# Hybrid encoder block, fp32 by split matmuls: w_o's Strassen groups end with P3, P4 in place of P4, P3, and three smaller moves of work on DVE and ACT

## The chip, the cores and the metric

The kernel runs on one core of a Trainium2 chip. The metric is the device time of one execution in microseconds. Before the change three runs took 2060.41, 2061.68 and 2065.68 us; the median is 2061.68. The engines are called as the profile calls them: PE is TensorE, DVE is VectorE, ACT is ScalarE, POOL is GpSimd, SP is SyncE, which issues most transfers.

## The reference

One layer of a streaming encoder on 1024 tokens of width 1024, all in fp32:

```python
def reference(x, ...):
    for l in range(DEPTH):
        h = h + FFN_RES_WEIGHT * swiglu_ffn(rmsnorm(h, norm_ffn1[l]), ffn1_w_in[l], ffn1_w_out[l])
        u = rmsnorm(h, norm_mix[l])
        ...
        h = h + W_o(sum_b sigmoid(gate_b) * branch_b)
        h = h + 0.5 * SwiGLU_2(RMSNorm(h))
    Final RMSNorm
```

(The last three lines stand in the reference's own words.) The mixing takes q, k, v, two gates and a pooling input from one projection of u; one branch is retention with rotary q and k and decay by head, the other a multi-scale trailing mean. `W_o` is a product of 1024 x 1024 with the merged branches. SwiGLU has an inner width of 2816.

## The kernel before

**Products.** Every fp32 operand is kept as a hi and a lo part (`split`, and `split_scaled` where a gain is folded in; lines 164 to 169), and one product is three matmuls, hi by hi (L184), hi by lo (L185) and lo by hi (L186). Tiles are 128 partitions by 512 tokens.

**Strassen groups.** The large products are made in 2 x 2 blocks of weights and operands by seven products in place of eight (`strassen`, from L470). Each of the seven is 4 blocks of k, so 12 matmuls. Their names here: P1 = L11 R11 and P2 = L12 R21 go into bank `a`; P6 = S2 T2, P5 = S1 T1 and P3 = S4 R22 go into bank `b`, which ACT starts with a copy of P1 (L529); P7 = S3 T3 and P4 = L22 T4 go into bank `e`. L and S are blocks of the weights or sums of them, R and T the same of the operand. Results leave the banks as follows: ACT copies `b` after P6 (the `v` of L534) and `e` after P7 (the `p7` of L551); output block (0,0) is `a` after P2, (1,1) is `b` after P5 plus p7, (0,1) is `b` after P3, and (1,0) is `e` after P4 plus v. There are two banks for `b` and six others.

**Order.** `two_by_two` runs two groups side by side, product by product. The order of the seven is a tuple of indices:

```python
BY_OPERAND = (0, 4, 1, 3, 2, 6, 5)
```

which reads P1, P2, P6, P7, P5, P4, P3. Weight preparation runs up to four steps ahead (`LOOK`). The other work (squares, operand sums T1 to T4, splits of operands, sums of norms) is put into a queue (`Flow`), of which two items are taken at each step. A scheduler then fixes the order in which each engine's instructions stand. DVE and ACT take them strictly as they stand there.

**w_o.** The stage has two pairs of groups, wo0 with wo1 and wo2 with wo3. The operand of the first is `mg`, the merged branches; it is made while the pair ru2, ru3 of the mixing's up-projections ends. `handed` decides which operand blocks are prepared after which product. `evac` takes the banks into `wo` tiles; for some blocks POOL adds h by a transfer (`onto`, L143), and the block's square for the norm of SwiGLU2 (named n3) is queued afterwards (`quarter`, then ACT's square, L291, and DVE's add into `n3ssq`, L303). After w_o, `stats` makes the norm's sums: PE adds over the partitions (`n3sum`), `inverse_root` takes the root (ACT, L241) and refines it on DVE, and `spread` makes rows of it. The result is the operand of SwiGLU2's first product, whose weight tiles are called c.

**Buffers.** Raw weight tiles (`ra`, `rb`, each 1024 wide and 0.5 MB) have four buffers; a new load goes out when the oldest one's last reader has finished. Split weights have five.

**Other places of the change.** `values` makes the product with w_v; in its loop over k, DVE makes sums of weights (L1332 to L1334) and their splits `vS1w` and `vS2w`. `rotary_tables` loads the cos and sin tables. ACT's functions lie in tables that are loaded when another is needed; there are ten loads in the program, among them L216 and L1190 at its start, L241 at each norm's root, L796 at the first SiLU and L1261 at the first sigmoid of the gates, which lies in the stretch of the tiles p1 and t1.

Of the kernel before, what the change touches and what calls it, by code (L numbers as in the profile page):

```python
# [10 lines left out]
F32 = mybir.dt.float32  # L11
F32R = mybir.dt.float32r  # L12
BF16 = mybir.dt.bfloat16
AF = mybir.ActivationFunctionType
# [3 lines left out]
P = 128  # L18
# [32 lines left out]
N_MV, N_T4, N_RAW, N_WT, N_TL, N_C2 = 28, 9, 4, 5, 4, 8  # L51
LOOK = 4

BY_OPERAND = (0, 4, 1, 3, 2, 6, 5)


class Flow:
# [28 lines left out]
    def add(self, *work):  # L86
        self.back.extend(work)
# [3 lines left out]
def block_kernel(ctx: ExitStack, tc, x, x_tok, x_two, vecs, f1_in, f1_out, w_in, w_v, pool_w, w_ret, w_pool, w_o,  # L91
# [8 lines left out]
    flow = Flow()  # L100
# [22 lines left out]
    def tl(name):  # L123
        return sb.tile([P, S], F32, tag="tl", bufs=N_TL, name=name)
# [24 lines left out]
    def spill(name, n, width=S):  # L149
        return [dr.tile([P, width], F32, tag=f"{name}{i}", name=f"{name}{i}") for i in range(n)]  # L150

    def half(t, j):
        return t[:, j * H : (j + 1) * H]
# [126 lines left out]
    class Norm:  # L280


        turns = False

        def __init__(self, name):
            self.name, self.ssq, self.seen = name, None, set()
# [6 lines left out]
        def square(self, mt, tokens, src):  # L293
            if self.ssq is None:
                self.ssq = t4(f"{self.name}ssq")
            dst = self.ssq[:, tokens]
            if tokens.start not in self.seen:
                self.squared(dst, src)
                self.seen.update(range(tokens.start, tokens.stop, HD))
            else:  # L300
                q = c2(f"{self.name}q{mt}_{tokens.start}")[:, : tokens.stop - tokens.start]
                self.squared(q, src)
                tt(dst, dst, q, ADD)  # L303

    class Next(Norm):
# [139 lines left out]
                for i in range(4):  # L445
                    flow.add(lambda f=f, i=i: f(i))

        def stats(self, sums=None, between=(), diagonals=None):
            def roots():
                t = sums if sums is not None else token_sums(self.ssq, range(8), self.name)  # L450
                self.r_tok = inverse_root(t, D, self.name)

            def row(q):
                if not q:
                    self.row = t4(f"{self.name}rb")
                to, b = half(self.row, q), spread(self.r_tok[:, 4 * q : 4 * q + 4], f"{self.name}{q}", diagonals)
                if sums is not None:
                    to, b = in_row(to), in_turns(b)
                copy(to, b)
                if q:  # L460
                    self.rb = self.row

            n = max(0, len(between) - 3)
            flow.add(roots, *between[:n], lambda: row(0), *between[n:], lambda: row(1))
# [722 lines left out]
        flow.until(lambda: stored.issuperset(names))  # L1187

    def rotary_tables():
        act(warm, warm, AF.Sigmoid)  # L1190
        for n, z in (("cos", 0), ("sin", 1)):
            tab[n] = t4(n)
            load(tab[n], rope[z])
            tt(tab[n], tab[n], mix.rms(), MUL)
# [108 lines left out]
    def values():  # L1303

        nx, kept, two, p1s = mix, {}, {}, {}

        def fetch(r, *rows):

            for z, (k, o) in enumerate(rows):
                load(half(r, z), w_v[k, :, o * H : (o + 1) * H])  # L1310
            return half(r, 0), half(r, 1)

        def rows(n, k):

            if (n, k // 2) not in two:
                at, o = k // 2 * 2 + (4 if n[2] == "2" else 0), (1 if n[1] == "2" else 0)
                two[n, k // 2] = fetch(raw(f"v{n}{k}"), (at, o), (at + 1, o))
            return two[n, k // 2][k % 2]

        def block(n, k):  # L1320

            if n[0] == "L":
                return rows(n, k)
            if n in ("S1", "S3"):
                return two.pop((n, k))

            L11 = rows("L11", k)
            if n == "S4":
                tt(L11, rows("L12", k), L11, SUB)
                return L11  # L1330
            L21, L22 = fetch(tl(f"v{n}{k}"), (k, 1), (k + 4, 1))
            tt(L22, L21, L22, ADD)  # L1332
            tt(L21, L11, L21, SUB)
            tt(L11, L22, L11, SUB)  # L1334
            two["S1", k], two["S3", k] = L22, L21
            return L11

        bk = {}

        def step(L, R, k, where, start, after):  # L1340
            w = []

            def prep():
                t = weights(block(L, k), f"v{L}w{k}")
                w.extend(in_turns(flat(t, z)) for z in range(2))

            def body():
                if start and k == 0:
                    for i in range(4):
                        bk[where, i] = (sum_bank if where == "b" and i < N_SUM else bank)(f"v{L}{i}")  # L1350
                m = nx.operand(R, k)
                for i in range(4):
                    mm3(bk[where, i], parts(m, slice(i * P, (i + 1) * P)), w, start and k == 0, k == 3)
                    if k == 3:
                        with soon():
                            after(i, bk[where, i])

            return prep, body

        def store(o, j, i, src):  # L1360
            to = vs[2 * o + j].rearrange("p (h t c) -> p h t c", h=2, t=4)
            load(to[:, :, i], src.rearrange("p (h c) -> p h c", h=2))
            if i == 3:
                stored.update(f"v{h}{j}" for h in (2 * o, 2 * o + 1))

        def keep(n, i):
            if i % 2 == 0:
                kept[n, i // 2] = t4(f"v{n}{i}")
            return half(kept[n, i // 2], i % 2)

        def old(n, i):
            return half(kept[n, i // 2], i % 2)

        def result(o, j, other=None):
            def after(i, b):
                c = c2(f"vc{o}{j}{i}")
                if other is None:
                    copy(c, b)
                else:
                    tt(c, b, other(i), ADD)  # L1380
                flow.add(lambda: store(o, j, i, c))
                if (o, j, i) == (0, 0, 3):
                    nx.stats(between=nx.blocks("R22", [("tl", N_TL)] * 3, True))

            return after

        def after1(i, b):
            p1s[i] = c2(f"vp1{i}")
            copy(p1s[i], b)

        def after6(i, b):
            copy(keep("h", i), b)

        def after5(i, b):
            copy(keep("f", i), b)

        def product(L, R, where, start, f):
            return [step(L, R, k, where, start, f) for k in range(4)]

        yield from product("L11", "R11", "a", True, after1)  # L1400
        s2, s1 = product("S2", "T2", "a", False, after6), product("S1", "T1", "b", True, after5)
        nx.work(nx.t3)
        for k in range(4):
            if k == 2:
                nx.work(nx.r21, nx.t4_)
            yield (lambda a=s2[k], b=s1[k]: (a[0](), b[0]())), s1[k][1]
            yield (lambda: None), s2[k][1]
        for p in zip(product("S4", "R22", "b", False, result(0, 1, lambda i: old("h", i))),
                     product("S3", "T3", "a", False, result(1, 1, lambda i: old("f", i)))):
            yield from p  # L1410
        yield from product("L12", "R21", "b", True, result(0, 0, lambda i: p1s.pop(i)))
        yield from product("L22", "T4", "a", False, result(1, 0))
# [438 lines left out]

        return [group(n, i) for n, i in enumerate(at)]

    waiting = []

    def out_group(i):
        pair = [None, None]
# [26 lines left out]

        return lambda: strassen(mg, w_o[i], w_o[i + 4], name, evac, none, begin)

    def handed(nx, last):

        f = after(nx)

        def between(pair, n):
            if n in (3, 5):
                flow.add(*waiting)
                waiting.clear()
            if pair == 0:
                if n == BY_OPERAND[-1]:
                    flow.add(*(lambda m=m, i=i: m(i) for i in range(2) for m in (nx.r22, nx.sum1, nx.sum3)))
                return
            flow.add(*(lambda i=i: f[n](i) for i in range(2)))

            for m in {3: (0,), 6: (4,)}.get(n, ()):
                flow.add(*(lambda i=i: f[m](i) for i in range(2, 4)))
            if n == BY_OPERAND[-1]:
                rest = [lambda m=m, i=i: f[m](i) for m in (1, 3, 2, 6, 5) for i in range(2, 4)]
                last(rest)

        return between

    def merge():
        yield from two_by_two(two_groups(0) + two_groups(1), BY_OPERAND, handed(mg, lambda rest: flow.add(*rest)))  # L1910
        yield from two_by_two((out_group(i) for i in range(4)), BY_OPERAND,
                              handed(ffn2, lambda rest: (flow.add(*rest[:4]), ffn2.stats(between=rest[4:]))))

    ffn2 = Next("n3", V_FFN2, h2)
    ops2 = spill("r2", FH), spill("t2", FH), spill("b2", FH), spill("m2", FH, H)

    class Last(Norm):
# [193 lines left out]
```

## Time and profile before

| what | value |
|---|---|
| median of 3 runs | 2061.68 us |
| the profiled execution | 2062.72 us |
| its span | 2060.9 us |
| granted clock of PE | 0.999 |
| w_o, 1375 to 1450 us: PE, DVE, ACT busy | 73.47, 71.60, 48.29 of 75.00 us |
| the rest up to 1375: PE busy | 472.19 of 475.00, then 894.99 of 900.00 |
| from 1450 on: PE, DVE busy | 599.90, 548.67 of 611.00 us |

The profile is one execution. Busy time is what an engine worked; matmuls overlap, so a busy PE need not be at its peak, and a matmul's listed duration (0.38 us) is longer than the step from one to the next. In the timeline a row has the start, the duration, engine, line, operation, `out<-in`, shapes, and in brackets the time that the engine idled before it with what released it. Buffer numbers are left out of names there.

### The profile page before, as it was taken

To read this page: it belongs to the slowest core of one execution; us is meant where nothing else is said; L and a number is where in the kernel's file an instruction comes from. 1 tells how busy PE (TensorE), PEld (TensorE's weight loads), DVE (VectorE), ACT (ScalarE), POOL (GpSimd) and SP (SyncE) were. 2 spreads that over 40 slices of the span, in tenths; PEclk is the share of its full clock that TensorE was granted. 3 is DMA by queue.
4 is the path that set the end of the run, shared out by engine and by line. 5 is a ranking of instruction groups with operands and counts; after the bars stand their busy time and mean duration, and the time that the engine had idled before them with its cause. 6 is when DMAs were issued, how large, how long until landed. Compare 5 with 4: busy or idle time off the path is not lost.

```text
span 2060.9 us, 29728 instructions
## 1 busy us (share of the span) xinstructions
PE 2040.5 (99%) x10672; PEld 1810.4 (88%) x10672; DVE 1831.2 (89%) x3253; ACT 1092.5 (53%) x2066; POOL 9.1 (0%) x14
## 2 busy tenths in 40 slices
PE   9999999999999999999999999999999999999998
PEld 7888999988888888888888999888889989998887
DVE  8889998998996798989789987899989989899896
ACT  8545454554754554454447753456645545455454
POOL 0000000000000000000000000010000000000000
PEclk9999999999999999999999999999999999999999
DMA  6332424585543333243337667545223232368642
GB/s 245 137 103 77 143 88 143 199 274 196 187 146 109 107 136 110 85 151 119 117 125 229 203 227 278 185 109 163 82 98 133 88 133 88 135 208 274 211 148 97
DMA packets 120260, 313.57 MB, mean 152 GB/s; under 512 B 13361, under 2 KB 17585, under 8 KB 120113
## 3 DMA queue, kind: packets, MB, share of 16 engines
q1 hardware_dynamic: 118096, 308.01, 43.9%
q0 software_dynamic: 1440, 2.62, 0.8%
q8 instruction: 83, 1.36, 0.3%
q10 hardware_dynamic: 576, 1.05, 0.1%
q14 instruction: 65, 0.52, 0.1%
HBM read 220.93 MB, written 90.70 MB: 151 GB/s over the span
## 4 chain that ended last, share of the span: by engine, by line
PE 81%; DVE 12%; DMA 2%; ACT 2%; issue 2%; SPq 0%; ACTq 0%; DVEq 0%
PE c_b L185 2%; PE c_b L184 2%; PE c_b L186 2%; PE a_b L184 2%; PE a_b L186 2%; PE a_b L185 2%; PE c_e L186 2%; PE c_e L184 2%; PE c_e L185 2%; PE a_e L186 1%; PE a_e L184 1%; PE a_e L185 1%; PE a_a L186 1%; PE a_a L185 1%; PE a_a L184 1%
## 5 line engine op out<-in xcount | busy, mean ns | idle before, releaser
L184 PE MATMUL c_b<-n3T,c_wS 128*128 128x512 f32 x176 | 66.8, 380 | 1.7 <-ACT n3T L164 1.7
L185 PE MATMUL c_b<-n3T,c_wS 128*128 128x512 f32 x176 | 66.8, 380 | 0.0
L186 PE MATMUL c_b<-n3T,c_wS 128*128 128x512 f32 x176 | 66.7, 379 | 0.0
L184 PE MATMUL a_b<-n1T,a_wS 128*128 128x512 f32 x168 | 63.7, 379 | 0.0
L185 PE MATMUL a_b<-n1T,a_wS 128*128 128x512 f32 x168 | 63.7, 379 | 0.0
L186 PE MATMUL a_b<-n1T,a_wS 128*128 128x512 f32 x168 | 63.7, 379 | 0.0
L184 PE MATMUL a_a<-n1R,a_wL 128*128 128x512 f32 x120 | 45.5, 379 | 0.0
L186 PE MATMUL a_a<-n1R,a_wL 128*128 128x512 f32 x120 | 45.5, 379 | 0.0
L185 PE MATMUL a_a<-n1R,a_wL 128*128 128x512 f32 x120 | 45.5, 379 | 0.0
L184 PE MATMUL c_a<-n3R,c_wL 128*128 128x512 f32 x112 | 42.7, 381 | 0.7 <-ACT c_b L529 0.5
L185 PE MATMUL c_a<-n3R,c_wL 128*128 128x512 f32 x112 | 42.4, 379 | 0.0
L186 PE MATMUL c_a<-n3R,c_wL 128*128 128x512 f32 x112 | 42.4, 379 | 0.0
L184 PEld LDWEIGHTS c_b<-n3T,c_wS 128*128 128x128 f32 x176 | 33.3, 189 | 6.6 <-ACT n3T L164 2.1
L185 PEld LDWEIGHTS c_b<-n3T,c_wS 128*128 128x128 f32 x176 | 33.3, 189 | 4.8 <-DVE n3T L165 0.3
L186 PEld LDWEIGHTS c_b<-n3T,c_wS 128*128 128x128 f32 x176 | 33.3, 189 | 4.7
L186 PEld LDWEIGHTS a_b<-n1T,a_wS 128*128 128x128 f32 x168 | 31.8, 189 | 4.5
L185 PEld LDWEIGHTS a_b<-n1T,a_wS 128*128 128x128 f32 x168 | 31.8, 189 | 4.4
L184 PEld LDWEIGHTS a_b<-n1T,a_wS 128*128 128x128 f32 x168 | 31.8, 189 | 4.4
L165 DVE TENSOR_TENSOR a_wS<-a_S,a_wS 128x512 fp32r<-128x512 f32 x45 | 30.7, 684 | 3.8 <-ACT a_wS L164 3.8
L165 DVE TENSOR_TENSOR c_wS<-c_S,c_wS 128x512 fp32r<-128x512 f32 x46 | 31.2, 681 | 2.6 <-ACT c_wS L164 2.6
L164 ACT CAST a_wS<-a_S 128x512 fp32r<-128x512 f32 x45 | 27.3, 621 | 11.7 <-PE a_a L186 6.1
L184 PE MATMUL c_e<-n3T,c_wS 128*128 128x512 f32 x88 | 33.5, 380 | 0.0
(3167 smaller groups left out, 8012.2 us busy)
## 6 DMA issues: line engine op xcount, KB each, us to landing
c_ra<-in_f_in SPq DMA_DIRECT2D x22, 512.0 KB, 3.6
c_rb<-in_f_in SPq DMA_DIRECT2D x22, 512.0 KB, 3.5
a_ra<-in_f_in SPq DMA_DIRECT2D x21, 512.0 KB, 3.7
a_rb<-in_f_in SPq DMA_DIRECT2D x21, 512.0 KB, 3.7
t<-au SPq DMA_DIRECT2D x11, 512.0 KB, 3.5
b<-ag SPq DMA_DIRECT2D x11, 512.0 KB, 4.1
r<-au SPq DMA_DIRECT2D x11, 512.0 KB, 3.7
bra<-in_f_out SPq DMA_DIRECT2D x11, 512.0 KB, 5.5
```

Of the source, the lines that this page charges most:

```text
L164: copy(hi, src)
L165: tt(lo, src, hi.bitcast(F32), SUB)
L184: mm(dst, w[0], m[0], start=start, stop=False, skip_group_check=True)
L185: mm(dst, w[0], m[1], start=False, stop=False, skip_group_check=True)
L186: mm(dst, w[1], m[0], start=False, stop=stop, skip_group_check=True)
```

## The change

Four things are changed.

1. w_o's groups run P1, P2, P6, P7, P5, P3, P4 (`BY_TURN`). `handed` and the new `settled` order the operand work by that: after P3 of the last pair T2 and T3 of the operand's blocks 2 and 3 are queued, and after P4 R21, R22, T1 and T4. For the hand-over from the mixing to w_o, whose groups still end with P4, P3, the splits of R22 of blocks 0 and 1 are queued after T2 and T3 rather than ahead of them.
2. Squares of w_o's blocks for n3 go into spare halves of other tiles (`aside`); DVE's adds of them are kept back in a list, of which two are queued after P1, P2, P6 and P5 of the second pair and the others at the end, one at a time, ahead of the norm's sums.
3. In `values` the R21 and T4 work of the next operand is queued after the loop over k and not in its third turn.
4. `stats` lets ACT evaluate one column of the norm's inverse with the function that is needed next (`then`: SiLU, for the mixing's norm the sigmoid). The sigmoid of a dummy tile in `rotary_tables` goes. ACT's program has nine table loads in place of ten.

The diff's core:

```diff
-BY_OPERAND = (0, 4, 1, 3, 2, 6, 5)
+BY_OPERAND, BY_TURN = (0, 4, 1, 3, 2, 6, 5), (0, 4, 1, 3, 2, 5, 6)
...
+            elif self.aside:
+                self.aside(mt, tokens, dst, src)
...
                 self.r_tok = inverse_root(t, D, self.name)
+                act(sb.tile([P, 8], F32, tag="st", bufs=10, name=f"{self.name}f")[:, :1], self.r_tok[:, :1], then)
...
     def rotary_tables():
-        act(warm, warm, AF.Sigmoid)
...
         for k in range(4):
-            if k == 2:
-                nx.work(nx.r21, nx.t4_)
             yield (lambda a=s2[k], b=s1[k]: (a[0](), b[0]())), s1[k][1]
             yield (lambda: None), s2[k][1]
+        nx.work(nx.r21, nx.t4_)
...
+    def aside(mt, tokens, dst, src):
+
+        if not spare:
+            q = tl(f"n3q{mt}_{tokens.start}")
+            spare.extend((half(q, 1), half(q, 0)))
+        q = spare.pop()
+        ffn2.squared(q, src)
+        apart.append(lambda: tt(dst, dst, q, ADD))
+
+    def add(n):
+        for _ in range(min(n, len(apart))):
+            apart.popleft()()
...
-            flow.add(*(lambda i=i: f[n](i) for i in range(2)))
-
-            for m in {3: (0,), 6: (4,)}.get(n, ()):
-                flow.add(*(lambda i=i: f[m](i) for i in range(2, 4)))
-            if n == BY_OPERAND[-1]:
-                rest = [lambda m=m, i=i: f[m](i) for m in (1, 3, 2, 6, 5) for i in range(2, 4)]
-                last(rest)
+            if nx is ffn2 and n in (0, 4, 1, 2):
+                flow.add(lambda: add(2))
+            if n != 5:
+                flow.add(*(lambda i=i: f[n](i) for i in range(2)))
+
+            for m in {3: (0,), 6: (4,), 5: (1, 3) if order[-1] != 5 else ()}.get(n, ()):
+                flow.add(*(lambda i=i, m=m: f[m](i) for i in range(2, 4)))
+            if n == order[-1]:
+                rest = [lambda m=m, i=i: f[m](i) for m, at in ((1, 2), (3, 2), (5, 0), (2, 2), (6, 2), (5, 2))
+                        for i in (at, at + 1)]
+                last(rest if n == 5 else rest[4:])
...
+        flow.add(more, *rest[:2])
+        ffn2.stats(between=rest[2:])
...
-        yield from two_by_two((out_group(i) for i in range(4)), BY_OPERAND,
-                              handed(ffn2, lambda rest: (flow.add(*rest[:4]), ffn2.stats(between=rest[4:]))))
+        yield from two_by_two((out_group(i) for i in range(4)), BY_TURN, handed(ffn2, settled, BY_TURN))
```

Three places show how instructions move. First DVE at the hand-over to w_o, before; `wo0wS2` and `wo1wS2` are the lo halves of the S2 weights that P6 of wo0 and wo1 read, `mgT2*` and `mgT3*` are splits of T2 and T3, `mgR22*` of R22, and the `ru` rows make the T sums:

```order
L165 TENSOR_TENSOR wo0wS2_13645<-wo0S2_13643,wo0wS2_13645 128x512
L351 TENSOR_TENSOR ru20_13292<-ru21_13294,mgt12_13667 128x512
L351 TENSOR_TENSOR ru30_13328<-ru31_13330,mgt13_13673 128x512
L492 TENSOR_TENSOR wo1S1_13679<-wo1rb_13563 128x512
L165 TENSOR_TENSOR mgT22_13670<-ru20_13292,mgT22_13670 128x512
L165 TENSOR_TENSOR mgT23_13676<-ru30_13328,mgT23_13676 128x512
L492 TENSOR_TENSOR wo1S2_13681<-wo1S1_13679,wo1ra_13562 128x512
L351 TENSOR_TENSOR ru20_13292<-ru21_13294,ru20_13292 128x512
L351 TENSOR_TENSOR ru30_13328<-ru31_13330,ru30_13328 128x512
L165 TENSOR_TENSOR wo1wS2_13683<-wo1S2_13681,wo1wS2_13683 128x512
```

The same stretch of DVE now:

```order
L165 TENSOR_TENSOR wo0wS2_13654<-wo0S2_13652,wo0wS2_13654 128x512
L165 TENSOR_TENSOR mgT32_13677<-ru20_13295,mgT32_13677 128x512
L353 TENSOR_TENSOR ru30_13331<-ru31_13333,ru30_13331 128x512
L495 TENSOR_TENSOR wo1S1_13684<-wo1rb_13566 128x512
L508 TENSOR_TENSOR wo0rb_13543<-wo0ra_13542,wo0rb_13543 128x512
L165 TENSOR_TENSOR mgT33_13681<-ru30_13331,mgT33_13681 128x512
L495 TENSOR_TENSOR wo1S2_13686<-wo1S1_13684,wo1ra_13565 128x512
L165 TENSOR_TENSOR mgR220_13710<-ru01_12945,mgR220_13710 128x512
L165 TENSOR_TENSOR mgR221_13713<-ru11_12988,mgR221_13713 128x512
L165 TENSOR_TENSOR mgT12_13734<-mgt12_13638,mgT12_13734 128x512
L165 TENSOR_TENSOR wo1wS2_13688<-wo1S2_13686,wo1wS2_13688 128x512
```

Before the row of `wo1wS2` stand now T3's splits, wo0's S3 (`wo0rb`), R22 and one split of T1; counted from the row that takes (0,1) of ru3 (`ru3h01<-ru3b`), it has moved from the 17th to the 21st place.

Second, PE where P5 of wo1 ends, before:

```order
L186 MATMUL wo1b<-mgT_13731,wo1wS_13786 128x512
L184 MATMUL wo1b<-mgT_13734,wo1wS_13786 128x512
L185 MATMUL wo1b<-mgT_13734,wo1wS_13786 128x512
L186 MATMUL wo1b<-mgT_13734,wo1wS_13786 128x512
L184 MATMUL wo0e<-mgT_13586,wo0wL_13803 128x512 [waits Activation_49]
L185 MATMUL wo0e<-mgT_13586,wo0wL_13803 128x512
```

and now:

```order
L186 MATMUL wo1b<-mgT_13734,wo1wS_13789 128x512
L184 MATMUL wo1b<-mgT_13737,wo1wS_13789 128x512
L185 MATMUL wo1b<-mgT_13737,wo1wS_13789 128x512
L186 MATMUL wo1b<-mgT_13737,wo1wS_13789 128x512
L184 MATMUL wo0b<-mgR_13710,wo0wS_13807 128x512 [waits DVE_49,Activation_49]
L185 MATMUL wo0b<-mgR_13710,wo0wS_13807 128x512
```

P3 of wo0 (`wo0b<-mgR`, R22) has come to the place of P4 (`wo0e`, L22). It writes the bank that P5 of wo0 wrote just ahead of these rows, and its first matmul waits for DVE.

Third, DVE from the evacuation of (1,1) of the last pair on, now (`c0` and `c11` are the first weights of SwiGLU2):

```order
L1888 TENSOR_TENSOR wo21_13982<-wo2b_13997,wo2p7_14137 128x512
L165 TENSOR_TENSOR wo3wL22_14194<-wo3rb_13912,wo3wL22_14194 128x512
L1888 TENSOR_TENSOR wo31_14011<-wo3b_14026,wo3p7_14164 128x512
L165 TENSOR_TENSOR c0_wL11_14221<-c0_ra_14217,c0_wL11_14221 128x512
L495 TENSOR_TENSOR c11_S1_14326<-c11_rb_14240 128x512
L1894 TENSOR_TENSOR wo20_13980<-wo2b_13997,wo20_13980 128x512
L165 TENSOR_TENSOR c11_wL11_14243<-c11_ra_14239,c11_wL11_14243 128x512
```

The last reader of wo3's rb, whose buffer c11's rb takes, is the second row, and the reader of c11's rb the fifth. Before the change the reader stood 18 rows behind the evacuation of wo3, and that buffer was freed well ahead of it. The splits of T2's block 2 (`n3T22`) stood 37 rows behind that evacuation and stand now 15 behind it.

More of the change, by code (lines that the diff above doesn't have):

```diff
@@ L280, in block_kernel @@
     class Norm:
-        turns = False
+        turns, aside = False, None
         def __init__(self, name):
@@ L446, in work, with stats @@
                     flow.add(lambda f=f, i=i: f(i))
-        def stats(self, sums=None, between=(), diagonals=None):
+        def stats(self, sums=None, between=(), diagonals=None, then=AF.Silu):
             def roots():
@@ L1382, in after @@
                 if (o, j, i) == (0, 0, 3):
-                    nx.stats(between=nx.blocks("R22", [("tl", N_TL)] * 3, True))
+                    nx.stats(between=nx.blocks("R22", [("tl", N_TL)] * 3, True), then=AF.Sigmoid)
             return after
@@ L1852, in two_groups @@
         return [group(n, i) for n, i in enumerate(at)]
-    waiting = []
+    waiting, spare, apart = [], [], deque()
+    def aside(mt, tokens, dst, src):
[8 more added lines that the diff above has]
+            apart.popleft()()
     def out_group(i):
@@ L1885, in out_group, with handed @@
         return lambda: strassen(mg, w_o[i], w_o[i + 4], name, evac, none, begin)
-    def handed(nx, last):
+    def handed(nx, last, order=BY_OPERAND):
         f = after(nx)
@@ L1895, in between, with settled, more @@
             if pair == 0:
-                if n == BY_OPERAND[-1]:
+                if n == order[-1]:
                     flow.add(*(lambda m=m, i=i: m(i) for i in range(2) for m in (nx.r22, nx.sum1, nx.sum3)))
                 return
-            flow.add(*(lambda i=i: f[n](i) for i in range(2)))
-            for m in {3: (0,), 6: (4,)}.get(n, ()):
-                flow.add(*(lambda i=i: f[m](i) for i in range(2, 4)))
-            if n == BY_OPERAND[-1]:
-                rest = [lambda m=m, i=i: f[m](i) for m in (1, 3, 2, 6, 5) for i in range(2, 4)]
-                last(rest)
-        return between
+            if nx is ffn2 and n in (0, 4, 1, 2):
[4 more added lines that the diff above has]
+                flow.add(*(lambda i=i, m=m: f[m](i) for i in range(2, 4)))
+            if n == order[-1]:
+                rest = [lambda m=m, i=i: f[m](i) for m, at in ((1, 2), (3, 2), (5, 0), (2, 2), (6, 2), (5, 2))
+                        for i in (at, at + 1)]
+                last(rest if n == 5 else rest[4:])
+        return between
+    def settled(rest):
+        def more():
+            add(1)
+            if apart:
+                flow.back.appendleft(more)
+        flow.add(more, *rest[:2])
+        ffn2.stats(between=rest[2:])
     def merge():
         yield from two_by_two(two_groups(0) + two_groups(1), BY_OPERAND, handed(mg, lambda rest: flow.add(*rest)))
-        yield from two_by_two((out_group(i) for i in range(4)), BY_OPERAND,
-                              handed(ffn2, lambda rest: (flow.add(*rest[:4]), ffn2.stats(between=rest[4:]))))
+        yield from two_by_two((out_group(i) for i in range(4)), BY_TURN, handed(ffn2, settled, BY_TURN))
     ffn2 = Next("n3", V_FFN2, h2)
+    ffn2.aside = aside
     ops2 = spill("r2", FH), spill("t2", FH), spill("b2", FH), spill("m2", FH, H)
```

## The prediction

> **What bounds the kernel now.** I read the page first, then the waits of PE, then the timeline where they lie.
>
> ```profile
> span 2060.9 us, 29728 instructions
> PE 2040.5 (99%) x10672; PEld 1810.4 (88%) x10672; DVE 1831.2 (89%) x3253; ACT 1092.5 (53%) x2066; POOL 9.1 (0%) x14
> ```
>
> PE works 2040.5 of 2060.9 us, so everything that waits could be taken away and the kernel would win 20.4 us at the most. The change touches no matmul, so it can only move these waits. The waits of PE name them (engine, line, waited for: us in total, times, longest):
>
> ```profile
> PE ru1a L184 <- ACT ru1b L529: 1.8, 1, 1.8
> PE c_b L184 <- ACT n3T L164: 1.7, 1, 1.7
> PE wo2a L184 <- ACT wo2b L529: 1.3, 1, 1.3
> PE t1b L184 <- ACT t1v L534: 0.9, 1, 0.9
> PE c_a L184 <- ACT c_b L529: 0.5, 1, 0.5
> PE vS L185 <- DVE vS1w L165: 0.5, 1, 0.5
> PE wo0e L186 <- DVE wo0wS L165: 0.2, 1, 0.2
> ```
>
> All but the first lie in places that the change touches. This view lists idle time alone. A wait also spoils the start of the matmuls behind it, as the one of wo0e shows in the timeline of PE (start, duration, engine, line, operation):
>
> ```profile
> 1390.98 0.38 PE L185 MATMUL wo0e<-mgT,wo0wS 128*128 128x512 f32 x1
> 1391.54 0.48 PE L186 MATMUL wo0e<-mgT,wo0wS 128*128 128x512 f32 x1 [0.18 <-DVE wo0wS L165]
> 1391.86 0.38 PE L184 MATMUL wo0e<-mgT,wo0wS 128*128 128x512 f32 x1
> 1398.77 0.38 PE L186 MATMUL wo0b<-mgT,wo0wS 128*128 128x512 f32 x1
> 1436.64 0.38 PE L186 MATMUL wo2b<-mgT,wo2wS 128*128 128x512 f32 x1
> ```
>
> From 1391.86 to 1398.77 stand 32 matmuls, 0.216 us each; a product of 12 takes 2.59 us. From 1390.98 to 1391.86, two steps take 0.88 in place of 0.43: 0.45 lost where 0.18 is listed. I add 0.27 for the restart to every listed wait. So the waits of w_o cost 0.45 (wo0e) + 1.57 (wo2a) = 2.0, and those of the start of SwiGLU2 come out of these rows:
>
> ```profile
> 1454.77 0.38 PE L186 MATMUL c_a<-n3R,c_wL 128*128 128x512 f32 x1
> 1455.69 0.48 PE L184 MATMUL c_a<-n3R,c_wL 128*128 128x512 f32 x1 [0.53 <-ACT c_b L529]
> 1458.16 0.38 PE L186 MATMUL c_a<-n3R,c_wL 128*128 128x512 f32 x1
> 1458.67 0.48 PE L184 MATMUL c_a<-n3R,c_wL 128*128 128x512 f32 x1
> ```
>
> 0.53 + 0.27 = 0.8 and 0.51 − 0.22 = 0.3 for the copies c_b, 1.97 for n3T: 3.1. In all, 5.1 us. Who sets the pace there is seen in the busy times of 1364 to 1482 us (width; busy of PE, PEld, DVE, ACT, POOL; clock; DMA):
>
> ```profile
> 1364.00:1482.00 118.00, 114.08 (x531) 98.16 (x530) 113.09 (x192) 76.96 (x141) 6.98 (x8) 1.00 0.45 131
> ```
>
> DVE is as full as PE (113.1 and 114.1 of 118). Here the order in DVE's queue decides which result is late.
>
> **The change part by part.** All sums are made as differences to the profiled execution (2062.72 us: its span and 1.8 around it), which lies 1.04 above the median of 2061.68; the difference is put on the median. Positions in a queue are counted in the order of the changed program; durations are from the trace.
>
> *Hand-over from the mixing to w_o.* The R22 splits of blocks 0 and 1 move behind T2 and T3. Anchors:
>
> ```profile
> 1376.83 0.68 DVE L1844 TENSOR_TENSOR ru3h<-ru3b,rg 128x512 f32<-128x512 f32 x1
> 1387.19 0.69 DVE L165 TENSOR_TENSOR wo1wS<-wo1S,wo1wS 128x512 fp32r<-128x512 f32 x1
> 1388.58 0.38 PE L186 MATMUL wo1b<-mgT,wo1wS 128*128 128x512 f32 x1
> ```
>
> Between the first two stand 17 steps, 0.61 us each. Afterwards there are 21, so the lo half of wo1's S2 starts at 1389.64 and ends at 1390.33. The matmul that reads it was due at 1388.58: 1.7 us of wait in place of the 0.45 at wo0e, whose weights follow in the next row. PE comes 1.25 later.
>
> *w_o with P3 ahead of P4.* P3 adds into the bank of P5. In the order of before P4 of both groups lay between; now P3 of a group comes right after P5 of its partner, 2.59 us later, and its first matmul waits until DVE has taken (1,1) out of that bank. How far DVE is behind is in these rows; the POOL transfer, ACT's squares and a weight load put it further behind:
>
> ```profile
> 1401.04 0.69 DVE L1880 TENSOR_TENSOR wo<-wo0b,wo 128x512 f32<-128x512 f32 x1
> 1439.82 0.68 DVE L1874 TENSOR_TENSOR wo<-wo2b,wo2p 128x512 f32<-128x512 f32 x1
> 1388.77 0.86 POOL L143 DMA_DIRECT2D wo<-h  x1 [2.74 <-ACT wo L1876]
> wo<-h POOLq DMA_DIRECT2D x2, 256.0 KB, 4.3
> 1413.19 0.75 ACT L291 ACTIVATE n3q<-wo 128x512 f32<-128x512 f32 x1 [0.85 <-DVE wo L1880]
> 1417.47 0.62 ACT L164 CAST wo2wS<-wo2S 128x512 fp32r<-128x512 f32 x1 [1.42 <-DVE wo2S L492]
> 1417.99 0.58 ACT L529 COPY wo2b<-wo2a 128x512 f32<-128x512 f32 x1
> wo2rb<-in_w_o SPq DMA_DIRECT2D x1, 512.0 KB, 4.8
> DVE n3ssq L303 <- ACT n3q L291: 2.6, 6, 0.9
> ```
>
> - Today's lag: P5 of wo0 ends at 1398.77 + 0.38 = 1399.15, DVE starts 1.89 later and needs 0.69: 2.58, just within 2.59. At wo2, 1439.82 − 1437.02 + 0.68 = 3.48: 0.9 too much.
> - wo0: ACT now squares wo1's (1,0) block directly after its copy, so it waits for the transfer that adds h: 1388.77 + 4.3 = 1393.1. Square and cast behind it, 0.75 + 0.62, give 1394.5 for wo1's S3, where DVE by its rows (six after 1389.64) would be at 1393.3: 1.2 idle. The evacuation is 13 rows later, at 1402.4, and ends at 1403.1; PE wants the bank at 1401.58 (1398.77 + 0.22 + 2.59) + 1.25 = 1402.8. Stall 0.3 + 0.27, say 0.5.
> - wo1: three rows on, DVE needs wo2rb. Its buffer is freed eight rows after 1394.5, at 1400.1, and 4.8 of landing make 1404.9 where DVE is ready at 1404.2. Two rows later wo1's evacuation runs from 1406.1 to 1406.8, wanted at 1402.8 + 0.5 + 2.6 = 1405.9: 1.2 with the restart.
> - wo2a, P2: the first group's sums are free 5.2 us earlier (24 matmuls), but the copy wo2b stands in ACT's queue behind a square of wo1 that waits for DVE. By that order 0.5 of the 1.57 stays.
> - wo2: from wo0's evacuation there were 58 rows, now 62; of the 2.6 us that DVE waits for squares, all but the longest wait (0.9, after this place) can go. 1402.4 + 38.8 (1439.82 − 1401.04) + 2.4 − 1.7 = 1441.9, end 1442.6. PE wants it at 1439.45 (1436.64 + 0.22 + 2.59), later by 1.25 + 0.5 + 1.2 and earlier by the 1.07 won at wo2a: 1441.3. That is 1.3 + 0.27 = 1.5 if the squares' waits go and 3.2 if they stay. I take 2.0, nearer to the former, since the adds are queued one product later.
> - wo3: DVE is there two rows (1.2 us) later, PE 2.59: nothing.
>
> *Start of SwiGLU2.* T2 and T3 come 15 rows after wo3's evacuation, 37 before: the 1.97 goes. Two things come instead.
>
> ```profile
> c_rb<-in_f_in SPq DMA_DIRECT2D x1, 512.0 KB, 3.5
> ```
>
> DVE's row that reads c11's rb stands three rows behind the one that frees its buffer: 0.7 + 3.5 − 1.8 = 2.4 idle. And the copies c_b stand behind ACT's casts of T2. DVE finishes the row for T2's last block 19 rows after the load, near 1459.4; cast and copy (0.62 + 0.58) end at 1460.5, wanted at 1454.99 (1454.77 + 0.22) + 3.9 (1.25 + 0.5 + 1.2 − 1.07 + 2.0) = 1458.9: 1.6. The second copy is four casts later and has half a product (1.3) of cover: about 1.2. R21's blocks 2 and 3, now behind T2 and T3, 0.5. Together 3.3, against 3.1. Bounds: 1.1 if the load is early (the two copies cost what they cost now), 5.7 if its 2.4 counts in full once more.
>
> w_o and the start of SwiGLU2: 1.7 + 0.5 + 1.2 + 0.5 + 2.0 + 3.3 = 9.2 in place of 5.1, **+4.1**. The 14 adds of squares are moved, not removed, and their sum is wanted one product later too, so they cost nothing by themselves.
>
> *Values.* The R21 and T4 rows go out of DVE's way:
>
> ```profile
> 624.43 0.69 DVE L165 TENSOR_TENSOR vS1w<-vS,vS1w 128x512 fp32r<-128x512 f32 x1
> 630.25 0.38 PE L184 MATMUL vS<-vS1w,n2T 128*128 128x512 f32 x1
> 630.72 0.48 PE L185 MATMUL vS<-vS1w,n2T 128*128 128x512 f32 x1
> ```
>
> The first wait of vS (0.51 + 0.27 = 0.8) ends with the split at 624.43. As many rows lie ahead of that split as before (eleven since the turn before it), so I leave it. The second, at 630.25 to 630.72, is 0.25 (0.47 less 0.22) and, with some restart, 0.4; it goes altogether, since its split now stands seven rows, over 4 us, earlier. R21 and T4 are read only after the loop's four turns. **−0.4** (bounds 0 and −1.2, both waits).
>
> *Function tables.* One load goes, three move to the norms.
>
> ```profile
> 731.84 1.28 ACT L1261 ACT_TABLE_LOAD   x1
> 733.14 0.84 ACT L1261 ACTIVATE t0z<-t0A,vec 128x512 f32<-128x512 f32 x1
> 734.52 0.69 DVE L165 TENSOR_TENSOR t1wS<-t1S,t1wS 128x512 fp32r<-128x512 f32 x1 [0.86 <-ACT t1wS L164]
> 740.67 0.59 ACT L534 COPY t1v<-t1b 128x512 f32<-128x512 f32 x1
> 4.09 0.62 ACT L164 CAST a_w<-ra 128x512 fp32r<-128x512 f32 x1 [0.34 <-DMA ra<-in_f_in]
> ```
>
> The load at 731.84 holds ACT 1.28 us and DVE behind it. Without it, and with one cast less ahead of the copy t1v (0.5), the copy comes up to 1.8 earlier, and the wait of t1b (0.91 + 0.27) goes: **−1.2** (bounds 0 and −1.2). The load that leaves the program's start wins nothing, since the cast behind it waits for its data until 4.09 anyway. The new places, behind the norms' roots, have slack of half a microsecond or more: 0.
>
> By the Trainium skill, "ScalarE: Activation LUTs", section "What ACT_TABLE_LOAD costs", a switch takes about 1.28 us for the load and some 1.38 more of drain, 2.66 in all. The trace agrees on the load, but the next activation starts 0.02 us after its end, so no drain shows. By that rule the load behind SwiGLU1's norm would overrun its slack by some 0.9 us (an estimate from that page), and the sum would be so much higher.
>
> **Sum:** +4.1 − 0.4 − 1.2 = +2.5; 2061.68 + 2.5 = **2064.2** (the profiled execution 2065.2).
>
> **The rivals.**
>
> A, all old waits go and none comes: −5.1 − 1.2 − 1.2 = −7.5, 2054.2. For it: P3 first does free the first pair's sums early, and DVE loses its waits for squares. Against: at wo2 even today's lag is above 2.59.
>
> B, slower: DVE's idle time is passed on in full. P3 waits for DVE in the bank of P5, and DVE waits for loads whose buffers are freed late; the three gaps, 1.2 + 0.7 + 2.4 = 4.3, come on top of the sum: 2068.5. It decides where DVE starts (1,1) more than 1.9 us (2.59 − 0.68) after P5 has ended, at three groups or four. For it: a lag of 1.89 and of 2.80 now. Against: PE's own delay at the hand-over gives DVE time back.
>
> C, w_o comes out even: the copies and P3 wait as long as T2 and wo2a did, and only values and t1b win: −1.6, 2060.1. It needs DVE no later at the hand-over than now, against the 21 rows.
>
> **How the numbers follow.** A measurement of this kernel tells about 0.3% (6.2 us) from no change: below 2055.5 is faster, above 2067.9 slower. Forecast 0.52, C 0.28, A 0.08, B 0.12. The forecast's own bounds: 3.2 for wo2 adds 1.2, SwiGLU2's 5.7 adds 2.4, and no gain in values and t1b 1.6; values, wo2 and SwiGLU2 at their low ends take 0.8 + 0.5 + 2.2 = 3.5. The range goes from C with SwiGLU2's and values' low ends (2060.1 − 2.2 − 0.4) to just above B's price, which leaves out A and the upper half of B: 2057.5 to 2069.0. Faster 0.08, within 0.3% 0.80, slower 0.12.
>
> **What would show it.** Right: in the waits of PE, wo1b <- DVE wo1wS near 1.5; wo0b, wo1b and wo2b <- DVE wo at first matmuls of P3; no c_b <- n3T, but two waits for copies; no t1b <- t1v; DVE idle for c_rb near 1445. Wrong: a PE busy share that rises with w_o's waits below 3 us in all (A or C), or more than 13 us of wait from 1375 to 1482 (B).

## The result, and the profile after

The changed kernel takes 2070.96 us (median of 6, 2067.51 to 2074.88) beside 2061.65 for the kernel before (6 runs, 2060.02 to 2065.68): 1.0039 times as long [1.0028, 1.0049]. It is slower by 9.3 us in the medians, where 2.5 were forecast. The profiled execution took 2074.88 us (span 2073.1), 12.2 more than the profiled one of before; it is the longest of the six. One execution in a later experiment (P4 ahead of P3) took 2558.63 us at a granted clock of 0.78 and is left out of the median given there.

The page's line of busy times for the changed kernel:

```profile
PE 2047.8 (99%) x10672; PEld 1813.8 (87%) x10672; DVE 1832.4 (88%) x3253; ACT 1091.5 (53%) x2067; POOL 9.1 (0%) x14
```

PE has the same 10672 matmuls, but is busy 7.3 us longer (2047.8 against 2040.5). So 12.2 more of span are 4.9 of idle time and 7.3 in which PE counts as busy for longer; a halved clock, shown below, makes 4.4 of these. The waits of PE, whole program:

```profile
PE wo2b L184 <- DVE wo L1888: 2.9, 1, 2.9
PE c_a L184 <- ACT c_b L532: 2.8, 2, 2.0
PE ru1a L184 <- ACT ru1b L532: 1.6, 1, 1.6
PE ob L186 <- DVE sm L165: 1.6, 1, 1.6
...
PE wo1e L184 <- ACT wo1wS L164: 1.0, 1, 1.0
PE wo1b L184 <- DVE wo L1894: 0.8, 1, 0.8
PE wo0b L184 <- DVE wo L1894: 0.8, 1, 0.8
...
PE wo1b L184 <- ACT wo1wS L164: 0.6, 1, 0.6
```

All three first matmuls of P3 that were named wait for DVE, the copies c_b have taken the place of n3T, and t1b and wo2a are gone from the head of the list. `wo1e` is new and was not foreseen. The first matmul of `wo1b` waits for ACT's cast (0.6), and only the third for DVE's row (0.4), where the prediction had DVE alone. `ob` lies in the retention, ahead of w_o; its wait was 0.2 before, and over the profiled executions of the kernels with the changed values and tables it lies between 0.2 and 1.6. The same stretch as before in the busy times (width; PE, PEld, DVE, ACT, POOL; clock; DMA):

```profile
1364.00:1482.00 118.00, 108.72 (x470) 90.62 (x469) 104.89 (x170) 69.20 (x122) 6.98 (x8) 0.96 0.41 116
```

DVE is busy 104.9 of 118 where it was busy 113.1, and does 170 pieces of work in place of 192: it is not overloaded, it waits. And the granted clock is 0.96 where it was 1.00. What DVE waits for, from 1375 to 1482:

```profile
DVE c_S L495 <- DMA c_rb<-in_f_in: 4.1, 1, 4.1
DVE wo1wS L165 <- ACT wo1wS L164: 3.1, 1, 3.1
...
DVE wo2S L495 <- DMA wo2rb<-in_w_o: 0.4, 1, 0.4
```

These are the three gaps of the prediction (2.4, 1.2, 0.7): the first two were sized 1.7 and 1.9 too small. ACT's timeline shows the second one, the square of wo1's block (0,0) (the prediction and two expectations call it (1,0)), which waits for the transfer that adds h, with the cast for wo1's S3 behind it, and DVE's row that waits for that cast:

```profile
1395.56 0.74 ACT L291 ACTIVATE n3q<-wo 128x512 f32<-128x512 f32 x1 [4.25 <-DMA wo<-h]
1396.20 0.60 ACT L164 CAST wo1wS<-wo1rb 128x512 fp32r<-128x512 f32 x1
```

```profile
1396.84 0.69 DVE L165 TENSOR_TENSOR wo1wS<-wo1rb,wo1wS 128x512 fp32r<-128x512 f32 x1 [3.07 <-ACT wo1wS L164]
```

The first one, in the timelines of SP and DVE: the load is issued as DVE's row for wo3wL ends, which frees its buffer. The reader stands three rows behind that row, and the data are there 5.2 us after the issue.

```profile
1447.42 0.33 SPq L140 DMA_DIRECT2D c_rb<-in_f_in  x1
```

```profile
1446.12 0.68 DVE L1888 TENSOR_TENSOR wo<-wo2b,wo2p 128x512 f32<-128x512 f32 x1
1446.72 0.68 DVE L165 TENSOR_TENSOR wo3wL<-wo3rb,wo3wL 128x512 fp32r<-128x512 f32 x1
1447.32 0.68 DVE L1888 TENSOR_TENSOR wo<-wo3b,wo3p 128x512 f32<-128x512 f32 x1
1447.92 0.68 DVE L165 TENSOR_TENSOR c_wL<-c_ra,c_wL 128x512 fp32r<-128x512 f32 x1
1452.65 0.69 DVE L495 TENSOR_TENSOR c_S<-c_rb 128x512 f32<-128x512 f32 x1 [4.05 <-DMA c_rb<-in_f_in]
```

And PE is slow after its long waits. PE's timeline where P3 of wo2 begins, and where the second copy c_b ends a wait:

```profile
1446.94 0.62 PE L184 MATMUL wo2b<-mgR,wo2wS 128*128 128x512 f32 x1 [2.90 <-DVE wo L1888]
1447.36 0.63 PE L185 MATMUL wo2b<-mgR,wo2wS 128*128 128x512 f32 x1
...
1450.35 0.47 PE L186 MATMUL wo2b<-mgR,wo2wS 128*128 128x512 f32 x1
...
1466.39 0.48 PE L184 MATMUL c_a<-n3R,c_wL 128*128 128x512 f32 x1 [1.98 <-ACT c_b L532]
...
1467.57 0.61 PE L186 MATMUL c_a<-n3R,c_wL 128*128 128x512 f32 x1
1468.97 0.80 PE L184 MATMUL c_a<-n3R,c_wL 128*128 128x512 f32 x1 [0.79 <-ACT c_b L532]
...
1474.25 0.46 PE L184 MATMUL c_a<-n3R,c_wL 128*128 128x512 f32 x1
```

From 1446.94 to 1450.35 stand 8 matmuls, 0.426 us each where 0.216 is the full rate: 1.7 lost. From 1468.97 to 1474.25 stand 12 in 5.28 us: 2.7 lost. The granted clock of these two stretches (same columns as above):

```profile
1447.00:1450.00 3.00, 3.00 (x8) 2.37 (x9) 1.60 (x3) 0.00 (x0) 1.74 (x2) 0.52 0.80 164
1469.00:1474.00 5.00, 5.00 (x12) 4.01 (x13) 5.00 (x9) 3.88 (x7) 0.00 (x0) 0.50 0.00 0
```

So 4.4 us of this execution went to a halved clock; before the change no matmul of this stretch ran at it. The Trainium skill, "TensorE: Matmul & The Clock Gate", section "Part 1: The HAM clock gate", says that the clock halves after an idle window of about 3.4 us and returns after as long of work. The first return agrees (3.41 us from 1446.94 to 1450.35), the second took longer (5.28); the way in differs: here 2.9 us of idle were enough, and so were 2.0 and 0.8 with six matmuls between.

The copies c_b have a square ahead of them as well. In ACT's timeline at the start of SwiGLU2 the last of w_o's squares waits for DVE, and the first copy stands behind it:

```profile
1464.57 0.74 ACT L291 ACTIVATE n3q<-wo 128x512 f32<-128x512 f32 x1 [1.36 <-DVE wo L1896]
...
1465.75 0.58 ACT L532 COPY c_b<-c_a 128x512 f32<-128x512 f32 x1
```

Before the change four squares stood behind that copy, the last of them at 1459.06:

```profile
1455.05 0.58 ACT L529 COPY c_b<-c_a 128x512 f32<-128x512 f32 x1
...
1459.06 0.75 ACT L291 ACTIVATE n3q<-wo 128x512 f32<-128x512 f32 x1
```

For all that follows, "lost steps" is the time by which the starts of PE's matmuls from 1365 to 1502 us stand further apart than 0.2155 us, summed over the timeline of one profiled execution: 5.5 before, 17.1 after, 11.6 more. With 1.5 won at values and t1b and 1.4 given back at `ob`, that is 11.5 of the 12.2.

### The profile page after: what moved, and what is told of

It is laid out like the page before. It is cut to its first block, busy times and chain, and to the rows that moved or that the text cites. A ratio compares the mean times of both kernels' runs of the same rounds, so it can differ in the third digit from the quotient of the medians.

```text
span 2073.1 us, 29720 instructions
## 1 busy us (share of the span) xinstructions
PE 2047.8 (99%) x10672; PEld 1813.8 (87%) x10672; DVE 1832.4 (88%) x3253; ACT 1091.5 (53%) x2067; POOL 9.1 (0%) x14
## 4 chain that ended last, share of the span: by engine, by line
PE 82%; DVE 9%; issue 4%; DMA 3%; ACT 2%; SPq 0%; POOL 0%; ACTq 0%; DVEq 0%; POOLq 0%
PE c_b L184 2%; PE c_b L185 2%; PE a_b L184 2%; PE c_b L186 2%; PE a_b L185 2%; PE a_b L186 2%; PE a_e L186 2%; PE c_e L186 2%; PE c_e L184 2%; PE a_e L184 2%; PE a_e L185 2%; PE c_e L185 2%; PE a_a L184 1%; PE a_a L185 1%; PE a_a L186 1%
## 5 line engine op out<-in xcount | busy, mean ns | idle before, releaser
L184 PE MATMUL c_e<-n3T,c_wL 128*128 128x512 f32 x88 | 33.4, 380 | 0.0
```

Of the source, the lines that this page charges most:

```text
L184: mm(dst, w[0], m[0], start=start, stop=False, skip_group_check=True)
```

## The experiments

The theory after the result: the new orders and the squares together put DVE's rows so that its idle gaps (c_rb, wo1wS) reach PE, as in rival B of the prediction. Its rivals: the turn of P3 and P4 does it alone; the squares do it alone, by their spare buffers or by the late sums; the halved clock does it, whatever brings the waits. Letters in the expectations stand for these and narrower ones, as each text says. "Measured" is the median of 5 to 11 executions in us, with the ratio to the kernel before on the same chip and its 95% interval.

**The two halves.** First values, tables and norms alone, put into the kernel before; second the rest alone, with these taken out of the changed kernel:

```
         for k in range(4):
-            if k == 2:
-                nx.work(nx.r21, nx.t4_)
...
+        nx.work(nx.r21, nx.t4_)
...
+                act(sb.tile([P, 8], F32, tag="st", bufs=10, name=f"{self.name}f")[:, :1], self.r_tok[:, :1], then)
...
-        act(warm, warm, AF.Sigmoid)
```

> The kernel before with only the moves in values and in the function tables (3 and 4 of the change). Theory W (all that is lost lies in w_o and the start of SwiGLU2): the waits of vS and t1b shrink by 0.6 and 0.9 us, so 2060.2, or up to 2062 if retention's pool weights, which landed no earlier in the changed kernel, take it back. Rival E (the loss lies elsewhere in the program): 2063 or more.

Measured: 2061.76, ratio 0.9999 [0.9990, 1.0008]. Its trace has no t1b among the waits of PE any more, yet the median is that of before.

> The changed kernel without the moves in values and tables: only w_o's order, the operand work and the squares. Theory W: 2071 to 2073, with waits for DVE at P3 of wo0, wo1, wo2 and for the copies c_b as in the changed kernel. Rival E: 2062 to 2064.

Measured: 2071.79, ratio 1.0049 [1.0036, 1.0061]. The whole loss is in w_o, the hand-overs and the squares; DVE's gaps are 3.1 (c_rb) and 3.2 (wo1wS) again.

**The old hand-over** from the mixing to w_o, in the changed kernel:

```
-            if n != 5:
+            if n != 5 or nx is mg:
...
+                if nx is mg:
+                    rest = [lambda m=m, i=i: f[m](i) for m in (1, 3, 2, 6, 5) for i in range(2, 4)]
```

> The changed kernel with the operand work at the hand-over from the mixing to w_o in the order of before (R22 ahead of T2 and T3). Theory W splits its loss: the hand-over's own waits (wo1b 1.5, wo1e 1.6 with restarts) go, the P3 waits and those of c_b stay: 2067 to 2069. Rival H (the hand-over alone starts it all): 2062 or less.

Measured: 2068.14, 1.0030 [1.0018, 1.0041]. The waits of wo1b at P6 are gone, those of P3 stay (wo2b 2.8), c_rb's gap is 3.0; the gap at wo1wS falls from 3.1 to 1.4. Some 3 us come back, at most.

**P4 ahead of P3 again** in w_o, all else changed:

```
-        yield from two_by_two((out_group(i) for i in range(4)), BY_TURN, handed(ffn2, settled, BY_TURN))
+        yield from two_by_two((out_group(i) for i in range(4)), BY_OPERAND, handed(ffn2, settled))
```

> The changed kernel with w_o's groups ending P4, P3 as before; the hand-over, the squares put aside and all else stay. Theory W: the waits at P3 (0.9, 0.9, 3.1) and the 1.7 of half clock behind the last go, the waits at the start of SwiGLU2 partly: 2061 to 2065. Rival H: 2069 to 2071, since the order of P3 and P4 has no part in it.

Measured: 2068.12 (seven executions), 1.0027 [1.0016, 1.0038]. The waits of PE from 1370 to 1492:

```profile
PE c_a L184 <- ACT c_b L532: 3.4, 1, 3.4
PE wo1e L184 <- ACT wo1wS L164: 1.2, 1, 1.2
PE wo2a L184 <- ACT wo2b L532: 1.1, 1, 1.1
PE wo3a L184 <- ACT wo3b L532: 0.7, 1, 0.7
```

No P3 waits any more, and still two thirds of the loss: the turn of P3 and P4, which the change is named after, is not its cause by itself.

**PE kept busy** ahead of wo2's P3, with 12 matmuls into a bank that nobody reads:

```
...
+            if name == "wo2":
+                idle(12)
             prod("b", "S4", "R22", False, True)
```

> The changed kernel with 12 matmuls of no use (2.6 us, into a bank of their own, with S1 and T1 of wo2 as operands) ahead of P3 of wo2, where PE idled 3.1 us and then ran eight matmuls at half the rate. Theory C (the idle time itself makes PE run at half rate for some microseconds): P3 starts no later, the eight matmuls step by 0.216 in place of 0.427, so 1.7 us less: 2069.3, granted clock 1.0 in the 3 us behind. Rival: the half rate comes of something else (supply of weights, the store of results), it stays, and the time is 2071 or more.

Measured: 2073.59, 1.0057 [1.0043, 1.0070]. PE's timeline at the place (the first row holds the last six of the twelve), and the waits of DVE:

```profile
1442.73 1.46 PE L566 MATMUL wo2f<-mgT,wo2wS 128*128 128x512 f32 x6
1444.52 0.45 PE L184 MATMUL wo2b<-mgR,wo2wS 128*128 128x512 f32 x1 [0.34 <-DVE wo L1897]
1444.82 0.38 PE L185 MATMUL wo2b<-mgR,wo2wS 128*128 128x512 f32 x1
```

```profile
DVE c_S L495 <- DMA c_rb<-in_f_in: 7.9, 1, 7.9
```

With the wait filled, P3 runs at the full rate: it is the idle time that halved the clock there. But nothing was won, since the load of c_rb now stood on SP behind a store of h, which waited for the transfer that adds h; its buffer had been free since 1445.58:

```profile
1449.64 0.32 SPq L140 DMA_DIRECT2D h<-wo  x1
1450.05 0.38 SPq L140 DMA_DIRECT2D c_rb<-in_f_in  x1
```

DVE idles 7.9 us, and the copies c_b let PE wait 6.3. How much the halved clock costs the median is not shown by this. The mean granted clock of each execution bounds it (0.001 of it is some 2 us): of the six of the result, that of 2071.31 us has 0.999, as the profiled one of before, and the fastest, of 2067.51, has 0.998. So most of the loss is there without it.

**c_rb's load early.** Two edits to give c11's two tiles buffers of their own, so that the load need not wait for wo3wL. The first:

```
-            ra, rb = raw(f"{name}ra"), raw(f"{name}rb")
+            to = tl if name == "c11" else raw
+            ra, rb = to(f"{name}ra"), to(f"{name}rb")
```

> The changed kernel with the raw weights of c11, the second group of SwiGLU2's first pair, in two buffers of another kind that are free earlier, so that their loads need not wait for wo2's and wo3's L22 splits. Theory L (the late load makes DVE idle 4.1 us, and by that the copies c_b wait and PE's clock falls): DVE's idle time there goes, of the 2.2 + 1.3 us of waits and 2.6 us of half rate at the start of SwiGLU2 at least 3 go: 2065 to 2068. Rival Q (the copies wait for the queue of ACT, whose squares wait for POOL's transfers): 2070 to 2071.

The weights are named `c11_`, so this edit changed nothing, and the run is the changed kernel once more: 2070.60, 1.0044 [1.0031, 1.0057], a second measurement of the result. Its profiled execution took 2068.60 us, with 14.2 of lost steps and 5 matmuls at the halved clock: how long the clock is down differs from one execution to the next. The second, with `"c11_"`:

> The changed kernel with the raw weights of c11 really in two buffers of another kind (in the run before this one the test of the group's name did not match, so that was the changed kernel again). Theory L (the late load starts the waits of the copies c_b): DVE's idle time for c_rb, 3.9 to 4.1 us, goes, and of the 2.2 + 1.3 us of waits and up to 2.6 us of half rate behind it at least 2 go: 2066 to 2069. Rival Q (the copies wait for ACT's queue with its squares): 2070 to 2072.

Measured: 2068.69, 1.0029 [1.0018, 1.0041], before 2062.76. The gap for c_rb is gone, and others stand in its place, in the waits of DVE:

```profile
DVE wo1wS L165 <- ACT wo1wS L164: 3.7, 1, 3.7
DVE wo L355 <- ACT wo L348: 3.0, 1, 3.0
```

PE waits 1.3 in place of 2.9 at wo2b, and 2.7 for a copy c_b. So c_rb's gap is worth some 3 us at most; the rest of the loss is there without it. Both edits together:

> The changed kernel with c11's early load and with the 12 matmuls of no use ahead of P3 of wo2. Alone these won nothing in the median, since the start of SwiGLU2 waited for c_rb all the longer. Theory C (half rate after an idle stretch costs 1.7 us there, and it was only given back at the load): 1.5 to 2.5 us below the kernel with the early load alone. Rival: half rate costs nothing that counts: the same.

Measured: 2071.84, 1.0048 [1.0034, 1.0062], 3 us worse than the early load alone, whose own wait at wo2b was only 1.3: filling does not pay here either.

**The squares as before** (each waits for a shared buffer, its sum follows at once), the orders changed:

```
-    ffn2.aside = aside
```

> The changed kernel with w_o's squares in the buffers and with the adds of before; P3, P4 and the operand work stay as changed. Theory S (free buffers let ACT take the square of wo1's (1,0) up before the cast of wo1's S3, where it waits for POOL's transfer, and DVE with it): the wait of wo1e (1.2 + 0.3 us) and DVE's idle 3.1 us go, and the waits at P3, now 0.9, 0.9 and 3.1, shrink with them: 2065 to 2068. Rival: the squares' place has no part in it, and the order of P3 alone holds PE: 2070 to 2072.

Measured: 2064.51, 1.0011 [1.0002, 1.0019]. This one line takes most of the loss away. ACT's timeline shows how: the cast for wo1's S3 no longer has the square ahead of it, which comes 7.6 us after it, as it came 6.1 after it in the kernel before (cast at 1392.12, square at 1398.24).

```profile
1389.98 0.62 ACT L164 CAST wo1wS<-wo1rb 128x512 fp32r<-128x512 f32 x1 [1.28 <-DVE wo1rb L508]
...
1397.59 0.74 ACT L291 ACTIVATE n3q<-wo 128x512 f32<-128x512 f32 x1
```

The waits of PE from 1370 to 1492:

```profile
PE c_b L185 <- DVE n3T L165: 1.3, 1, 1.3
PE wo2b L184 <- ACT wo3wL L164: 1.2, 1, 1.2
PE c_a L184 <- ACT n3R L168: 0.9, 1, 0.9
PE wo2a L184 <- ACT wo2b L532: 0.7, 1, 0.7
PE wo1b L184 <- ACT wo1wS L164: 0.6, 1, 0.6
```

No wo1e, no P3 that waits for DVE, no gap for c_rb, and the wait for a copy c_b is 0.5. The first copy has two squares behind it on ACT again. That goes through the runs: with squares aside, all of them stand ahead of the first copy (but for the two runs with the early load) and PE waits 2.1 to 6.3 us for the copies; with squares as before, two to four stand behind it and PE waits 0.5 to 0.7. No run moves these squares alone, so their share of that wait is read from the order.

**Squares aside, both orders as before** (the two edits of the old hand-over and of P4 ahead of P3 together; for SwiGLU2's operand R22 of blocks 0 and 1 stays behind T2 and T3):

> The changed kernel with both the old hand-over and P4, P3 in w_o; squares put aside and late adds, values and tables stay. If the two parts add (each alone won 2.8 us): 2065 to 2066, 3 to 4 us above the kernel before, which would then be the squares' own price. If they won the same microseconds twice: 2068.

Measured: 2063.63, 1.0004 [0.9995, 1.0013]. The squares alone cost nothing that can be told from zero. **The new turn alone** (the old hand-over, and the squares as before) completes the set:

> P3, P4 in w_o with the new operand order there, the hand-over and the squares as before; values and tables as changed. With the squares as before, P3, P4 and the new hand-over together cost 1.8 us. The new hand-over's wait at wo1b is 1.5 us with restarts, so without it 2061 to 2063.5: the order of P3 and P4 alone neither wins nor loses. If P3 right behind P5 is dear by itself: 2065 or more.

Measured: 2064.30, 1.0013 [1.0004, 1.0021].

**Aside for the last pair alone**, which tells wo1's gap from c_rb's:

```
-            elif self.aside:
+            elif self.aside and mt % 4 > 1:
```

> The changed kernel with squares put aside for the last pair of w_o alone (wo2, wo3); those of wo0 and wo1 have the buffers and adds of before. Theory S1 (the square of wo1's (1,0), taken up ahead of a cast and waiting for POOL, starts the chain): wo1e's wait and DVE's 3.1 us of idle go, the P3 waits of wo0, wo1, wo2 shrink, 2064 to 2067. Theory S2 (the squares of the last pair, ahead of the copies c_b at the start of SwiGLU2, are what costs): 2069 to 2071, or at most the 1.6 of wo1e less.

Measured: 2068.40, 1.0035 [1.0021, 1.0049]. The waits at wo1e and in the first pair's P3 are gone, c_rb's gap is 2.5, and the copy c_b costs 3.1. The last pair carries most of the loss; 2.7 (9.3 − 6.6) is left to the first, and the two intervals overlap.

**Buffers or late sums?** The squares keep their spare buffers, but each sum is queued at once:

```
-        apart.append(lambda: tt(dst, dst, q, ADD))
+        tt(dst, dst, q, ADD)
```

> The changed kernel with squares in the spare halves as changed, but each add into the sums queued with its square and not kept back. Theory B (the spare buffers alone do it: squares come early in ACT's queue, and on DVE the reader of c11's rb moves up to three rows behind the row that frees its buffer; it stands three rows behind it here too): DVE idles 3 us or more for c_rb, 2069 to 2072. Theory A (keeping the adds back does it: they are what DVE lacks during that load): the idle time shrinks below 2.5 us and the time comes down to 2065 to 2067.

Measured: 2071.38, 1.0044 [1.0030, 1.0058]. DVE waits 3.0 for c_rb and 3.1 at wo1wS, as in the changed kernel. So "squares added later" is not the cause; that a square has a buffer of its own is. It then stands earlier on ACT, as the timelines show.

All of it in one table (medians as differences to the kernel before of the same chip; lost steps of the profiled execution; by how many DVE rows the reader of c_rb stands behind the row that frees its buffer):

| orders, squares | ratio | us | lost steps | DVE rows |
|---|---|---|---|---|
| old, old (values and tables changed) | 0.9999 | 0.0 | 5.6 | freed well ahead |
| old, aside | 1.0004 | +0.9 | 8.6 | 9 |
| new, old | 1.0011 | +1.8 | 8.8 | 11 |
| new but for the hand-over, old | 1.0013 | +2.5 | 8.7 | 11 |
| new but for P3/P4, aside | 1.0027 | +6.4 | 12.4 | no gap |
| new, aside in the last pair | 1.0035 | +6.6 | 10.7 | 7 |
| new but for the hand-over, aside | 1.0030 | +6.4 | 12.7 | 3 |
| new, aside, sums at once | 1.0044 | +9.1 | 13.5 | 3 |
| new, aside (the change) | 1.0039 | +9.3 | 17.1 | 3 |

Without the squares aside the new orders cost at most 2.5 us, without the new orders the squares aside cost 0.9; together they cost 9.3. No version is measurably faster than the kernel before.

## Why the prediction was wrong

By its own steps, in lost time of PE in the trace, restarts included as in the forecast:

| term | forecast | trace |
|---|---|---|
| wo1b at the hand-over | 1.7 | 1.5 |
| wo1e | 0 | 1.6 |
| P3 of wo0, wo1 | 0.5, 1.2 | 1.0, 1.0 |
| copies to wo2a, wo3a | 0.5, 0 | 0.3, 0.3 |
| P3 of wo2 | 2.0 | 3.1 |
| copies c_b | 3.3 with R21 | 2.2 and 1.2 |
| halved clock | not in the sum | 4.4 |
| values and t1b | −1.6 | −1.5, in the median 0 |

Without the last row the forecast's terms come to 9.2 and the trace's to 16.6. Of the 7.4 between them 4.4 are the halved clock, 1.6 wo1e and 1.1 P3 of wo2.

- **What held.** That DVE's order decides, that PE waits at the hand-over (though the first part of it is for ACT's cast), that P3 waits in the bank of P5 at three of four groups, that the copies c_b replace n3T, that the early function load wins nothing, and that the three gaps of DVE lie at wo1wS, wo2rb and c_rb.
- **The step that failed** is "The 14 adds of squares are moved, not removed, and their sum is wanted one product later too, so they cost nothing by themselves." The adds do cost nothing (sums at once: the same time). But what the edit changes is the squares ahead of them: with spare buffers they rise on ACT above the casts (and, at the start of SwiGLU2, above the copies c_b), and the reader of c_rb stands 3 rows behind the row that frees its buffer where it stands 11 with the squares as before. By the runs with and without, the buffers make 7.5 us of the 9.3, as long as the new orders are there. The prediction had the square ahead of the cast in its working, for 1.2 of DVE's time and no wait at wo1e, and did not ask what the stretch would be with the square behind it.
- **Sizes.** The block of h was forecast for 1393.1 and came at 1395.56: POOL issued the transfer 0.7 later than before, and it took 6.1 in place of 4.3. So the gap was 3.1 in place of 1.2. The c_rb load took 5.2 us in place of the 3.5 of before, and the gap was 4.1 in place of 2.4. Both prices were taken from the trace of the kernel before. With the forecast's 1394.5 for the cast, wo1e would have been served in time; PE was ready for it 1.2 us before it could start.
- **A term that was missing.** 4.4 us of halved clock in the profiled execution. The forecast counted 0.27 for a restart whatever the length of the wait, since before's own longest, 1.8 at ru1a, shows no more. In the second profile of the same kernel, which took 2068.60, only some 5 matmuls ran at it, so it differs between executions.
- **Values and tables.** The waits went as worked out, and the median did not move. What took the gain back stays open. The wait at ob, in the retention, is 1.6 in the profiled execution of the change, but 0.2 in that of values and tables alone, as in the kernel before, so it is not shown to come from them.
- **The rivals.** B named the mechanism, DVE's idle time passed on, and the side; its price of 2068.5 is 2.5 under the median, since the gaps were larger than the 4.3 it added and the clock was not in it. Its deciding point was right: three of four groups were late. A and C fell with the waits of P3.

Left open: how much the halved clock costs the median, since the kernels with the wait filled got longer waits elsewhere; how the spare buffers close up DVE's rows for the last pair, step by step; what besides the length of the idle time decides whether the clock falls; and what took back the gain of values and tables.

## What to carry to other kernels

A spare buffer is a change of order: it lets an instruction rise past whatever it used to wait behind, so ask what on its engine now stands behind it, and what that one's transfer waits for. Count, for each load that reuses a buffer, the rows between the one that frees it and the one that reads it: 9 or more covered the landing here, 7 or fewer did not. And two edits that each use up slack are tried together before either is called free, here 0.9 and 1.8 us each alone and 9.3 together.

## What was not expected of the hardware

- PE's clock halved after 2.9 us of idle time, and after 2.0 and 0.8 close together, for 3.4 and 5.3 us; a wait of 2.74 in the run with the early load left it at full rate, while one of 2.81 in the run with squares aside and old orders, and one of only 2.61 in the second profile of the changed kernel, did not. So the length of the wait alone does not decide:

```profile
1463.05 0.48 PE L184 MATMUL c_a<-n3R,c_wL 128*128 128x512 f32 x1 [2.74 <-ACT c_b L533]
```

```profile
1458.34 0.80 PE L184 MATMUL c_a<-n3R,c_wL 128*128 128x512 f32 x1 [2.81 <-ACT c_b L532]
1458.93 0.63 PE L185 MATMUL c_a<-n3R,c_wL 128*128 128x512 f32 x1
```

```profile
1444.53 0.76 PE L184 MATMUL wo2b<-mgR,wo2wS 128*128 128x512 f32 x1 [2.61 <-DVE wo L1889]
```

- The transfer that adds h to a block, issued by POOL at 1389.50, let ACT's square begin at 1395.56, 6.1 us later; before, such transfers took 4.3 in the median.

```profile
1389.50 0.86 POOL L143 DMA_DIRECT2D wo<-h  x1 [3.27 <-ACT wo L1890]
```

- A load that is queued on SP behind a store that is not ready goes with it: c_rb was issued 2.6 us later (1450.05 in place of 1447.42) though PE and DVE were earlier, and DVE's wait for it rose from 4.1 to 7.9.
